# RMSNorm with silu on 16384 rows: hand-placed waits on one program per engine instead of a scheduler

## The chip, the cores and the metric

One core of a Trainium2 chip. The time is device time of the slowest core, here of the only one, in microseconds (us). The kernel before took 185.58 us (median of 3 runs, 185.26 to 185.62). Engines: ACT is ScalarE, DVE is VectorE, POOL is GpSimd, SP only issues transfers and waits. A trailing q ("ACTq") is the engine's queue of issues.

## The reference, cut to what matters

```python
x: (16, 1024, 512) float32, gamma: (512,) float32, eps = 1e-5
rms    = sqrt(mean(x**2, axis=-1, keepdims=True) + eps)
x_norm = x / rms * gamma
return x_norm * (1 / (1 + exp(-x_norm)))
```

The input is 33.55 MB and the output the same. The kernels cut it into 32 tiles of 128 partitions x 4 rows x 512, 1 MB each. A tile is loaded, squared and summed (three of its four rows on ACT, one on DVE), gets rstd = (mean + eps)^-0.5 on GpSimd, is multiplied by rstd and gamma on DVE ("norm"), goes through silu on ACT and is stored.

## The kernel before

The kernel names tiles and dependences; a scheduler puts each engine's instructions in order and places all waits.

```python
lead = 10
xpool = ctx.enter_context(tc.tile_pool(name="xbuf", bufs=20))
...
def load(t):
    x_t = xpool.tile([P, n, D], fp32, name="x_t")
    nc.sync.dma_start(out=x_t[:], in_=xv[t])              # L59
...
def store(t):
    nc.scalar.dma_start(out=ov[t], in_=xt.pop(t)[:])      # L106, on ACT's queue

load(0)
nc.scalar.dma_start(out=gamma_sb[:], in_=gamma.partition_broadcast(P))
for t in range(1, lead):
    load(t)
for k in range(T + 3):
    if k < T:
        stats(k); rstd(k)      # squares: ACT L68, DVE L74; mean: DVE L84; power: POOL L89
    if 0 <= k - 1 < T:
        norm(k - 1)            # DVE L96
    if 0 <= k - 2 < T:
        swish(k - 2)           # ACT L103
        store(k - 2)
    if k + lead < T:
        load(k + lead)
```

## Time and profile before

| | before |
|---|---|
| time, span of the profiled run | 185.58, 183.7 us |
| busy: DVE, ACT, POOL | 60%, 66%, 18% |
| bytes moved | 67.42 MB, of them 0.26 MB gamma |
| mean rate over the span | 367 GB/s |
| rate while the DMA engines are full | 427 GB/s |

No engine is near 100%, and the mean rate is 86% of the full rate. So averages do not tell what bounds this kernel; the slices of the span do, and the prediction shows them. Beside them, the sixth part of the page lists the transfers: the operation, how many, their size, and the median from issue to landing.

```profile
x_t<-in_x_dram SPq DMA_DIRECT2D x32, 1024.0 KB, 20.9
out_dram<-x_t ACTq DMA_DIRECT2D x32, 1024.0 KB, 8.8
```

Loads wait 20.9 us in a long queue, stores 8.8 us in a short one: the DMA engines take packets from both queues, and loads are far ahead.

### The profile page before, as it was taken

What the parts mean: (1) busy time and instruction counts of PE and PEld (TensorE: products, weight loads), DVE (VectorE), ACT (ScalarE), POOL (GpSimd) and SP (SyncE); (2) the same over time, 40 slices, a digit from 0 to 9 for tenths busy, and PEclk for the clock granted to TensorE, in tenths of its full rate; (3) what the DMA queues carried; (4) which work ended last, traced back from release to release, by engine and by line L of the source; (5) the groups of instructions that cost most, each with busy time, mean ns of one, the idle gap of its engine ahead of it and who ended that gap; (6) DMA issues with size and microseconds to landing.
All of it is one profiled execution on the core that took longest, in us unless ns stands there. A gap on an engine that the chain in (4) does not pass through costs nothing.

```text
span 183.7 us, 711 instructions
## 1 busy us (share of the span) xinstructions
DVE 110.7 (60%) x225; ACT 120.9 (66%) x225; POOL 32.8 (18%) x36
## 2 busy tenths in 40 slices
DVE  0177877777725527064443777777777777777650
ACT  2449988842572643168076987999988888888450
POOL 0022322222220201022022222222222222222200
DMA  5999999999999999999999999999985555555195
GB/s 178 338 428 428 425 426 428 423 426 426 428 425 426 423 426 428 425 426 428 428 426 428 428 426 428 428 425 426 425 359 234 228 228 228 228 228 228 57 400 230
DMA packets 9365, 67.42 MB, mean 367 GB/s; under 512 B 1040, under 2 KB 1040, under 8 KB 1168
## 3 DMA queue, kind: packets, MB, share of 16 engines
q10 hardware_dynamic: 4752, 33.82, 44.0%
q1 hardware_dynamic: 4608, 33.56, 44.0%
q14 instruction: 5, 0.04, 0.1%
HBM read 33.82 MB, written 33.55 MB: 367 GB/s over the span
## 4 chain that ended last, share of the span: by engine, by line
DMA 47%; DVE 26%; POOL 9%; issue 9%; ACT 5%; SPq 0%; ACTq 0%; POOLq 0%; DVEq 0%
DMA x_t<-in_x_dram 39%; DVE x_t L96 20%; POOL rstd L89 9%; DMA out_dram<-x_t 7%; DVE sq_dve L74 5%; ACT sq_act L68 3%; ACT x_t L103 2%; DVE aeps L84 1%; SPq L59 0%; ACTq L106 0%; POOLq L89 0%; DVE ms L74 0%; DVEq L96 0%; ACTq L68 0%
## 5 line engine op out<-in xcount | busy, mean ns | idle before, releaser
L96 DVE SCALAR_TENSOR_TENSOR x_t<-x_t,rstd,gamma_sb 128x512 f32<-128x512 f32 x128 | 87.8, 747 | 37.4 <-POOL rstd L89 37.4
L68 ACT ACTIVATE sq_act<-x_t 128x512 bf16<-128x512 f32 x96 | 59.0, 615 | 42.0 <-DMA x_t<-in_x_dram 41.9
L103 ACT ACTIVATE x_t<-x_t 128x2048 f32<-128x2048 f32 x32 | 60.8, 1901 | 15.3 <-DVE x_t L96 13.2
L89 POOL TENSOR_TENSOR rstd<-aeps,neg_half 128x4 f32<-128x4 f32 x32 | 32.6, 1020 | 141.1 <-DVE aeps L84 141.1
L74 DVE CUSTOM_DVE_ANT_0 sq_dve<-x_t 128x512 bf16<-128x512 f32 x32 | 21.9, 685 | 6.3 <-DMA x_t<-in_x_dram 6.3
L84 DVE TENSOR_SCALAR aeps<-ms 128x4 f32<-128x4 f32 x32 | 5.3, 166 | 21.8 <-ACT sq_act L68 21.8
L68 ACT ACTIVATION_READ_ACCUMULATOR sq_act<-x_t 128x1 f32 x96 | 17.9, 186 | 0.0
L74 DVE DVE_READ_ACCUMULATOR2_ANT ms<- 128x1 f32 x32 | 2.6, 83 | 0.0
L44 ACT ACT_TABLE_LOAD x1 | 1.3, 1283 | 0.7 <-PEq L139 0.7
L48 DVE MEMSET neg_half<- 128x4 f32 x1 | 0.1, 62 | 0.8 <-PEq L139 0.8
L139 POOL MEMSET const-float32-0.0<- 128x1 f32 x1 | 0.1, 99 | 0.2 <-issue 0.2
L139 POOL MEMSET const-bfloat16-1.0<- 128x1 bf16 x1 | 0.1, 102 | 0.0
L139 POOL MEMSET const-uint8-127<- 128x1 uint8 x1 | 0.1, 102 | 0.0
L139 POOL MEMSET const-float32-1.0<- 128x1 f32 x1 | 0.1, 99 | 0.0
## 6 DMA issues: line engine op xcount, KB each, us to landing
x_t<-in_x_dram SPq DMA_DIRECT2D x32, 1024.0 KB, 20.9
out_dram<-x_t ACTq DMA_DIRECT2D x32, 1024.0 KB, 8.8
gamma_sb<-in_gamma_dram ACTq DMA_DIRECT2D x1, 256.0 KB, 7.1
```

Of the source, the lines that this page charges most:

```text
L44: nc.scalar.preload_act_table_set("silu_and_others")
L48: nc.vector.memset(neg_half[:], -0.5)
L68: nc.scalar.activation(out=junk[:], in_=x_t[:, j, :], func=AF.Square, accum_out=ms[:, j : j + 1],)
L74: nc.vector.tensor_tensor_reduce(out=junk[:], in0=x_t[:, j, :], in1=x_t[:, j, :], scale=1.0, scalar=0.0, op0=ALU.mult, op1=ALU.add, accum_ ...
L84: nc.vector.tensor_scalar(out=aeps[:], in0=ms[:], scalar1=inv_d, scalar2=eps_f, op0=ALU.mult, op1=ALU.add,)
L89: nc.gpsimd.tensor_tensor(out=r[:], in0=aeps[:], in1=neg_half[:], op=ALU.pow)
L96: nc.vector.scalar_tensor_tensor(out=x_t[:, j, :], in0=x_t[:, j, :], scalar=r[:, j : j + 1], in1=gamma_sb[:], op0=ALU.mult, op1=ALU.mult,)
L103: nc.scalar.activation(out=x_t[:], in_=x_t[:], func=AF.Silu)
L139: nc = _bacc.Bacc("TRN2", target_bir_lowering=False, num_devices=1)
```

## The change

Its intent: take order and waits from the scheduler. Each engine runs one program in order; every slot has a semaphore of its own for its load and one for its store; SP issues loads and stores in alternation; DVE takes the norm of a tile one tile late, so that rstd has time; gamma is loaded into 4 partitions and spread by a shuffle.

```diff
-    lead = 10
+    lead = 8
+    slots = 20
...
+    ld = [tc.alloc_semaphore(f"ld{s}") for s in range(slots)]
+    st = [tc.alloc_semaphore(f"st{s}") for s in range(slots)]
...
     def load(t):
-        x_t = xpool.tile([P, n, D], fp32, name="x_t")
-        nc.sync.dma_start(out=x_t[:], in_=xv[t])
+        if t >= slots:
+            nc.sync.wait_ge(st[t % slots], 16 * (t // slots))
+        nc.sync.dma_start(out=X(t), in_=xv[t]).then_inc(ld[t % slots], 16)
+
+    def store(t):
+        nc.sync.wait_ge(s_swish, t + 1)
+        nc.sync.dma_start(out=ov[t], in_=X(t)).then_inc(st[t % slots], 16)
...
-    def store(t):
-        nc.scalar.dma_start(out=ov[t], in_=xt.pop(t)[:])
...
+        for t in range(lead):
+            load(t)
+        for t in range(T):
+            store(t)
+            if t + lead < T:
+                load(t + lead)
...
+        for t in range(T + 2):          # ACT
+            if t < T:
+                sum_act(t)
+            if t >= 2:
+                swish(t - 2)
+
+        for t in range(T + 1):          # DVE
+            if t < T:
+                sum_dve(t)
+                mean_eps(t)
...
+            if t >= 1:
+                norm(t - 1)
...
+        for s in range(slots):
+            nc.sync.wait_ge(st[s], 16 * ((T - 1 - s) // slots + 1))
```

More of the change, by code (lines that the diff above doesn't have):

```diff
@@ L36 @@
     ov = of.rearrange("(t p n) d -> t p n d", p=P, n=n)
-    consts = ctx.enter_context(tc.tile_pool(name="consts", bufs=1))
-    xpool = ctx.enter_context(tc.tile_pool(name="xbuf", bufs=20))
-    junk_a = ctx.enter_context(tc.tile_pool(name="junk_a", bufs=2))
-    junk_v = ctx.enter_context(tc.tile_pool(name="junk_v", bufs=2))
-    small = ctx.enter_context(tc.tile_pool(name="small", bufs=6))
-    nc.scalar.preload_act_table_set("silu_and_others")
-    gamma_sb = consts.tile([P, D], fp32)
-    neg_half = consts.tile([P, n], fp32)
@@ L48 @@
-    nc.vector.memset(neg_half[:], -0.5)
+    pool = ctx.enter_context(tc.tile_pool(name="all", bufs=1))
+    xb = pool.tile([P, slots, n, D], fp32, name="xb")
+    gamma4 = pool.tile([P, D], fp32, name="gamma4")
+    gamma_sb = pool.tile([P, D], fp32, name="gamma_sb")
+    junk_a = pool.tile([P, n, D], bf16, name="junk_a")
+    junk_v = pool.tile([P, n, D], bf16, name="junk_v")
+    neg_half = pool.tile([P, n], fp32, name="neg_half")
+    ms = pool.tile([P, T, n], fp32, name="ms")
+    aeps = pool.tile([P, T, n], fp32, name="aeps")
@@ L50 @@
+    rstd = pool.tile([P, T, n], fp32, name="rstd")
     inv_d = 1.0 / float(D)
     eps_f = float(eps)
-    xt: dict[int, bass.AP] = {}
-    ms_of: dict[int, bass.AP] = {}
-    rstd_of: dict[int, bass.AP] = {}
-    def load(t):
-        x_t = xpool.tile([P, n, D], fp32, name="x_t")
-        nc.sync.dma_start(out=x_t[:], in_=xv[t])
-        xt[t] = x_t
-    def stats(t):
-        x_t = xt[t]
-        ms = small.tile([P, n], fp32, name="ms")
-        for j in range(n):
-            if j < n_act:
-                junk = junk_a.tile([P, D], bf16, name="sq_act")
-                nc.scalar.activation(
-                    out=junk[:], in_=x_t[:, j, :], func=AF.Square,
-                    accum_out=ms[:, j : j + 1],
-                )
-            else:
-                junk = junk_v.tile([P, D], bf16, name="sq_dve")
-                nc.vector.tensor_tensor_reduce(
-                    out=junk[:], in0=x_t[:, j, :], in1=x_t[:, j, :],
-                    scale=1.0, scalar=0.0, op0=ALU.mult, op1=ALU.add,
-                    accum_out=ms[:, j : j + 1],
-                )
-        ms_of[t] = ms
@@ L81, in rstd @@
-    def rstd(t):
-        ms = ms_of.pop(t)
-        aeps = small.tile([P, n], fp32, name="aeps")
-        nc.vector.tensor_scalar(
-            out=aeps[:], in0=ms[:], scalar1=inv_d, scalar2=eps_f,
-            op0=ALU.mult, op1=ALU.add,
-        )
-        r = small.tile([P, n], fp32, name="rstd")
-        nc.gpsimd.tensor_tensor(out=r[:], in0=aeps[:], in1=neg_half[:], op=ALU.pow)
-        rstd_of[t] = r
-    def norm(t):
-        x_t = xt[t]
-        r = rstd_of.pop(t)
-        for j in range(n):
-            nc.vector.scalar_tensor_tensor(
-                out=x_t[:, j, :], in0=x_t[:, j, :], scalar=r[:, j : j + 1],
+    ld = [tc.alloc_semaphore(f"ld{s}") for s in range(slots)]
@@ new lines, with X @@
+    st = [tc.alloc_semaphore(f"st{s}") for s in range(slots)]
+    g_ld = tc.alloc_semaphore("g_ld")
+    s_const = tc.alloc_semaphore("s_const")
+    s_half = tc.alloc_semaphore("s_half")
+    s_gamma = tc.alloc_semaphore("s_gamma")
+    s_sum_a = tc.alloc_semaphore("s_sum_a")
+    s_sum_v = tc.alloc_semaphore("s_sum_v")
+    s_aeps = tc.alloc_semaphore("s_aeps")
+    s_rstd = tc.alloc_semaphore("s_rstd")
+    s_norm = tc.alloc_semaphore("s_norm")
+    s_swish = tc.alloc_semaphore("s_swish")
+    def X(t):
+        return xb[:, t % slots]
@@ new lines, in landed, with sum_act @@
+    def landed(eng, t):
+        eng.wait_ge(ld[t % slots], 16 * (t // slots + 1))
+    def load(t):
+        if t >= slots:
[4 more added lines that the diff above has]
+        nc.sync.dma_start(out=ov[t], in_=X(t)).then_inc(st[t % slots], 16)
+    def sum_act(t):
+        landed(nc.scalar, t)
+        if t > 0:
+            nc.scalar.wait_ge(s_sum_a, t)
+        for j in range(n_act):
+            ins = nc.scalar.activation(
+                out=junk_a[:, j, :], in_=X(t)[:, j, :], func=AF.Square,
+                accum_out=ms[:, t, j : j + 1],
+            )
+        ins.then_inc(s_sum_a, 1)
@@ new lines, in sum_dve, with mean_eps @@
+    def sum_dve(t):
+        landed(nc.vector, t)
+        if t > 0:
+            nc.vector.wait_ge(s_sum_v, t)
+        for j in range(n_act, n):
+            ins = nc.vector.tensor_tensor_reduce(
+                out=junk_v[:, j, :], in0=X(t)[:, j, :], in1=X(t)[:, j, :],
+                scale=1.0, scalar=0.0, op0=ALU.mult, op1=ALU.add,
+                accum_out=ms[:, t, j : j + 1],
+            )
+        ins.then_inc(s_sum_v, 1)
+    def mean_eps(t):
+        nc.vector.wait_ge(s_sum_a, t + 1)
+        nc.vector.wait_ge(s_sum_v, t + 1)
+        nc.vector.tensor_scalar(
+            out=aeps[:, t, :], in0=ms[:, t, :], scalar1=inv_d, scalar2=eps_f,
+            op0=ALU.mult, op1=ALU.add,
+        ).then_inc(s_aeps, 1)
@@ L98, in norm, with root @@
+    def root(t):
+        nc.gpsimd.wait_ge(s_aeps, t + 1)
+        nc.gpsimd.tensor_tensor(
+            out=rstd[:, t, :], in0=aeps[:, t, :], in1=neg_half[:], op=ALU.pow
+        ).then_inc(s_rstd, 1)
+    def norm(t):
+        nc.vector.wait_ge(s_rstd, t + 1)
+        for j in range(n):
+            ins = nc.vector.scalar_tensor_tensor(
+                out=X(t)[:, j, :], in0=X(t)[:, j, :], scalar=rstd[:, t, j : j + 1],
                 in1=gamma_sb[:], op0=ALU.mult, op1=ALU.mult,
             )
+        ins.then_inc(s_norm, 1)
@@ L101, in swish @@
     def swish(t):
-        x_t = xt[t]
-        nc.scalar.activation(out=x_t[:], in_=x_t[:], func=AF.Silu)
-    def store(t):
-        nc.scalar.dma_start(out=ov[t], in_=xt.pop(t)[:])
-    load(0)
-    nc.scalar.dma_start(out=gamma_sb[:], in_=gamma.partition_broadcast(P))
-    for t in range(1, lead):
-        load(t)
-    for k in range(T + 3):
-        if k < T:
-            stats(k)
-            rstd(k)
-        if 0 <= k - 1 < T:
-            norm(k - 1)
-        if 0 <= k - 2 < T:
-            swish(k - 2)
-            store(k - 2)
-        if k + lead < T:
-            load(k + lead)
+        nc.scalar.wait_ge(s_norm, t + 1)
@@ new lines, in swish @@
+        nc.scalar.activation(out=X(t), in_=X(t), func=AF.Silu).then_inc(s_swish, 1)
+    with tc.tile_critical():
+        for t in range(lead):
[4 more added lines that the diff above has]
+                load(t + lead)
+        nc.gpsimd.memset(gamma4[:], 0.0).then_inc(s_const, 1)
+        nc.scalar.wait_ge(s_const, 1)
+        nc.scalar.dma_start(
+            out=gamma4[0:P:32, :], in_=gamma.partition_broadcast(4)
+        ).then_inc(g_ld, 16)
+        nc.scalar.preload_act_table_set("silu_and_others")
+        nc.gpsimd.memset(neg_half[:], -0.5).then_inc(s_half, 1)
+        nc.gpsimd.wait_ge(s_half, 1)
+        for t in range(T + 2):
[7 more added lines that the diff above has]
+                mean_eps(t)
+            if t == 0:
+                nc.vector.wait_ge(g_ld, 16)
+                nc.vector.stream_shuffle(gamma_sb[:], gamma4[:], [0] * 32).then_inc(s_gamma, 1)
+            if t == 1:
+                nc.vector.wait_ge(s_gamma, 1)
+            if t >= 1:
+                norm(t - 1)
+        for t in range(T):
+            root(t)
+        for s in range(slots):
+            nc.sync.wait_ge(st[s], 16 * ((T - 1 - s) // slots + 1))
```

## The prediction

> **What bounds the kernel now.** I read the page first, for where the time is not used. Its second part, the busy shares in 40 slices of 4.6 us:
>
> ```profile
> DVE  0177877777725527064443777777777777777650
> ACT  2449988842572643168076987999988888888450
> DMA  5999999999999999999999999999985555555195
> GB/s 178 338 428 428 425 426 428 423 426 426 428 425 426 423 426 428 425 426 428 428 426 428 428 426 428 428 425 426 425 359 234 228 228 228 228 228 228 57 400 230
> ```
>
> Three stages can be seen. Slices 0 and 1 are the start. In slices 2 to 28, up to about 133 us, the DMA engines are full at some 427 GB/s while both compute engines have holes, worst in slices 8 to 20. From slice 29 on the DMA engines are half empty at 228 GB/s and ACT and DVE are at 70 to 80%. So the kernel is first bound by transfers and then by compute, and the compute lost in the first stage is paid for in the last one. At 427 GB/s the 67.42 MB of the page's third part need 157.9 us; the other 26 us of the 183.7 us span are the start and the half-empty tail.
>
> Next the chain of work that ended last. In its middle:
>
> ```profile
> 31.44 23.19 DMA x_t<-in_x_dram
> 54.65 19.03 DMA x_t<-in_x_dram
> ...
> 74.16 23.56 DMA x_t<-in_x_dram
> 97.72 0.02 issue
> 97.76 0.04 issue
> 97.80 0.34 ACTq L106
> 98.14 0.05 issue
> 98.19 0.78 ACT sq_act L68 x3
> ```
>
> A load issued at 74.16 us lands at 97.72 us; what it releases is not the squares of its own tile but the *issue of a store* on ACT's queue (L106) at 97.80, and the squares (L68) come behind it. No data ties that store to that load. The instruction order explains it: the scheduler has only eight DMA semaphores, deals them out to loads and stores in turn, and lets each DMA wait until the previous DMA with its semaphore has landed. A store behind a load on the same semaphore holds ACT's in-order queue until that load lands. I went through the trace's landing times: the store issued at 66.37 us follows a load landing at 66.30, the one at 58.70 a load at 58.62, the one at 51.34 a load at 51.27. The view of waits sums this up:
>
> ```profile
> ACT sq_act L68 <- DMA x_t<-in_x_dram: 41.9, 13, 6.7
> ...
> DVE aeps L84 <- ACT sq_act L68: 21.8, 8, 5.8
> ```
>
> The 41.9 us "of ACT for loads" are, but for the first wait of some 5 us and one of 1 us, waits of a store for a semaphore and not for data: at 44 us eleven loads had landed and only six tiles were swished. Meanwhile loads run ahead to fill 20 buffers, so the DMA stays full but with the wrong half of its work: all loads have landed at 125.97 us, when about half of the stores are still to come.
>
> Last, what paces the tail. One period of the same chain:
>
> ```profile
> 147.76 2.07 DVE x_t L96 x3
> 149.83 0.60 DVE sq_dve L74
> 150.44 0.10 DVE aeps L84
> 150.54 0.02 issue
> 150.58 0.09 issue
> 150.67 1.02 POOL rstd L89
> 151.69 0.02 issue
> 151.71 0.04 DVE x_t L96
> ```
>
> The chain comes round every 4.62 us: DVE asks GpSimd for rstd of a tile and at once needs it for the norm of the *same* tile, so DVE idles about 1.2 us per tile (37.4 us in 32 waits over the kernel). One 1 MB store per 4.62 us is the 228 GB/s of the tail.
>
> **What the Trainium skill says.** "DMA: Bandwidth & Descriptors", section "Issuing engines are not separate DMA queues", says that DMAs started by SP and by ACT run on the same 16 DMA engines, and a second issuing engine saves issue time only. The trace agrees: loads alone (slices 2 and 3), both queues, and stores alone (landing every 2.4 to 2.8 us from 126 to 139 us) all move about 427 GB/s. So putting the stores on SP's queue should cost no bandwidth. The same page, "Where 436 GB/s comes from", derives a ceiling of 435.2 GB/s; 428 is 98% of it, so I expect no faster transfers, only fuller use. Its "Rules for kernel authors" advise a dedicated semaphore for a DMA, which is what the change does; the 41.9 us show what sharing costs here. All durations below come from the trace.
>
> **The change part by part.**
>
> *Semaphores per slot, stores issued by SP.* Removed: every wait of a DMA on an unrelated one. Loads now wait for the store that freed their slot 12 tiles earlier (long landed), stores for their own swish. ACT loses 32 store issues of 0.34 us and the roughly 36 us of false waits.
>
> *Order fixed by hand.* On DVE it is now sum(t), mean(t), norm(t-1), so rstd has about a period to come: the 1.2 us wait goes. DVE per tile: 0.685 (sum) + 0.17 (mean) + 4 x 0.69 (norms back to back, 2.74 in the timeline) = 3.6 us. ACT: three squares and one silu back to back took 3.63 us (21.14 to 24.77 us in the timeline); with hand-placed waits I take 3.7 to 3.9. Both are below the 1.0486 MB x 2 / 427 GB/s = 4.91 us that one load and one store need, so compute stops being a bound in every stage and the transfers must set the pace throughout.
>
> *Lead 8, load t+8 issued behind store t on one queue.* This binds loads to stores, so that they can't run ahead. Is 8 enough? Eight periods are 39.3 us. A tile spends on compute: two periods until tile t+2 has landed (ACT takes the squares of t+2 before the silu of t), 9.8 us, plus 1.9 and 1.9 us for these two, 13.6 us. About 25.7 us remain as queueing of a transfer, some ten transfers deep: the queue never runs dry. At the start eight loads fill it until about 25 us, and store 0 comes at about 17 us. At the end load 31 is the 56th of 64 transfers, lands near 142 us, and leaves eight stores, 19.6 us; its own compute needs about 10 us. The last store is ready near 153 us, before its turn at 159. So the engines should be full from about 9 us to the end.
>
> *Gamma.* 256 KB become 8 KB: 0.25 MB / 427 GB/s = 0.6 us of DMA less. In its place stand a GpSimd fill and a shuffle on DVE, under a microsecond or so each by the length of their 128x512 output, in the 7 us before the first tile or beside tile 0: nothing on the path.
>
> *Sum.* In the kernel before, load 5 landed at 20.02 us; six loads were then moved, plus gamma. 58 transfers of 2.456 us follow: 142.4 us. 20.0 + 142.4 - 0.6 = 161.8 us for the last landing. Before, the last store landed at 182.78 us and the span ended 0.9 us later: 162.7. I add 0.8 us for the barrier around the hand-written part and the slower completion of a store in a full queue (an estimate by feel): span 163.5 us. The timed value stands 1.9 us over the span (185.58 against 183.7): **165.4 us**, 11% less. The gain of 20 us consists of the tail: it was 54 us at about 228 GB/s, moving what 29 us at 427 would, 25 us lost, of which the last tile's compute and landing were never avoidable in full.
>
> **Rivals.** (1) *One ring is worse than two.* Loads and stores in alternation in one ring have not been seen in this trace; a turn between reading and writing HBM could cost. Against it: packets of both queues alternated in the first stage at 427 GB/s, each taking the same 309 ns. If each transfer lost 0.1 us, 64 x 0.1 = 6 us: 172 us. (2) *The queue's depth.* At most eight DMAs were outstanding before; now about ten would be in one ring. If SP blocks when the ring is full, it blocks with the DMA engines busy, so the time stays at 165 us; only landing times would be shorter than my 25 us. (3) *Compute becomes the bound.* If hand-placed waits drain ACT or DVE, a tile would have to cost 4.9 us instead of 3.8 before it shows; at 5.2 us per tile, 32 x 5.2 plus 10 us of start and 5 of end are 181 us. The self-waits number two or three per tile and cannot plausibly make 1.1 us. (4) *DMA was full already.* Reading only the first 29 slices, one would say that removing waits buys nothing: 185 us. Against it stands the tail, in which the engines are half idle.
>
> **Range and chances.** Below the 157.2 us of pure transfer plus the 5 us of start and 2 of launch lies nothing: the low end is 164.0. Rival 1 in a mild form gives the high end, 170.0. Faster by over 2% needs less than 181.9 us, which only rivals 3 and 4 in full miss: 0.96; within 2% 0.03; slower 0.01.
>
> **What would show it.** Right: about 427 GB/s in every slice from the third to the last but one; DMA share of the slices 9 throughout; all bytes on SP's queue (some 67.1 MB); loads and stores alike landing some 25 us after issue; DVE waiting for rstd hardly at all (below 5 us in place of 37.4); squares waiting some 1.2 us per tile, for their own load; silu busy until about 153 us with only stores after it. Wrong: slices below 415 GB/s in the middle (rival 1), DMA slices of 7 or 8 with ACT at 9 (rival 3), or a last stage of stores at less than full rate.

## The result, and the profile after

The changed kernel takes 166.81 us (median of 4 runs, 166.74 to 167.47), beside 185.42 us for the kernel before (now with a fourth run): a ratio of 0.9006, 95% interval 0.8978 to 0.9033.

The busy shares of the changed kernel in 40 slices, now of 4.1 us:

```profile
DVE  0269999999996666786666776666876666784000
ACT  3488999999977977777977758877778977777000
DMA  4999999999999999999999999999999999999990
GB/s 157 415 425 429 425 342 429 411 431 427 427 431 419 431 423 433 423 431 425 429 427 427 423 425 431 421 435 419 435 423 431 425 425 431 421 433 423 433 405 26
```

The three stages have become one. DMA is at 9 from the second slice to the last but one, loads and stores mixed. The compute engines are full only up to slice 10 or 11, while they work off the first loads, and then follow the transfers, DVE at 60 to 80% and ACT at 70 to 90%. The last load lands at 142.84 us, so from slice 35 on there are stores alone, at full rate.

One of the waits of the kernel before (engine and line, what it waited for, us in total, times, longest), and the longest two of ACT and DVE in the changed kernel:

```profile
DVE x_t L96 <- POOL rstd L89: 37.4, 32, 1.2
```

```profile
DVE aeps L107 <- ACT junk_a L86: 28.9, 26, 1.3
ACT junk_a L86 <- DMA xb<-in_x_dram: 26.9, 23, 2.0
```

DVE's wait for rstd, 37.4 us before, is not in the list of the changed kernel any more. ACT still waits for loads, 26.9 us, but 2.0 us at most at a time, and now for data of the tile it is about to square. One period of the timeline shows this (start, duration, engine, line, operation, then idle time before it and its releaser):

```profile
87.11 0.34 SPq L79 DMA_DIRECT2D out_dram<-xb  x1
87.50 1.42 SPq L75 DMA_DIRECT2D xb<-in_x_dram  x1
88.25 0.63 ACT L86 ACTIVATE junk_a<-xb 128x512 bf16<-128x512 f32 x1 [1.17 <-DMA xb<-in_x_dram]
...
90.10 1.89 ACT L129 ACTIVATE xb<-xb 128x2048 f32<-128x2048 f32 x1
90.23 0.17 DVE L107 TENSOR_SCALAR aeps<-ms 128x4 f32<-128x4 f32 x1 [1.28 <-ACT junk_a L86]
90.31 2.73 DVE L121 SCALAR_TENSOR_TENSOR xb<-xb,rstd,gamma_sb 128x512 f32<-128x512 f32 x4
90.48 1.44 POOL L114 TENSOR_TENSOR rstd<-aeps,neg_half 128x4 f32<-128x4 f32 x1 [3.48 <-DVE aeps L107]
92.02 0.34 SPq L79 DMA_DIRECT2D out_dram<-xb  x1
```

A store goes out every 4.9 us (87.11, 92.02), the time of two transfers. The norms (L121) start right behind the mean with no idle, because they use the rstd of the tile before. The power on GpSimd now takes 1.44 us against 1.01 to 1.02 us before. The Trainium skill, "SBUF — State Buffer", section "Who interferes with whom", says that a DVE instruction with two SBUF inputs contends with a GpSimd instruction that reads SBUF; the trace agrees in direction, as the norms have two inputs in SBUF and now run beside it (with the order undone, in old_dve_order below, the power's mean is back at 1.01 us). It has a whole period to end, so it costs nothing.

### The profile page after: what moved, and what is told of

Same layout as the page of the kernel before. It is cut to its first block, busy times and chain, and to the rows that moved or that the text cites. A ratio compares the mean times of both kernels' runs of the same rounds, so it can differ in the third digit from the quotient of the medians.

```text
span 165.0 us, 713 instructions
## 1 busy us (share of the span) xinstructions
DVE 112.0 (68%) x226; ACT 120.5 (73%) x225; POOL 46.4 (28%) x38
## 4 chain that ended last, share of the span: by engine, by line
DMA 63%; ACT 17%; issue 6%; DVE 5%; SPq 1%
DMA xb<-in_x_dram 63%; ACT junk_a L86 12%; ACT xb L129 6%; DVE xb L121 5%; SPq L79 1%; SPq L75 0%; DVE aeps L107 0%; SPq L203 0%; SPq L131 0%
## 5 line engine op out<-in xcount | busy, mean ns | idle before, releaser
L121 DVE SCALAR_TENSOR_TENSOR xb<-xb,rstd,gamma_sb 128x512 f32<-128x512 f32 x128 | 87.4, 745 | 0.0
L86 ACT ACTIVATE junk_a<-xb 128x512 bf16<-128x512 f32 x96 | 59.2, 617 | 26.9 <-DMA xb<-in_x_dram 26.9
L114 POOL TENSOR_TENSOR rstd<-aeps,neg_half 128x4 f32<-128x4 f32 x32 | 45.7, 1427 | 99.4 <-DVE aeps L107 99.4
L129 ACT ACTIVATE xb<-xb 128x2048 f32<-128x2048 f32 x32 | 60.6, 1895 | 2.2 <-DVE xb L121 2.2
L97 DVE CUSTOM_DVE_ANT_0 junk_v<-xb 128x512 bf16<-128x512 f32 x32 | 22.0, 689 | 8.7 <-DMA xb<-in_x_dram 6.8
L86 ACT ACTIVATION_READ_ACCUMULATOR junk_a<-xb 128x1 f32 x96 | 17.9, 186 | 0.0
L162 DVE STREAM_SHUFFLE gamma_sb<-gamma 128x512 f32<-128x512 f32 x1 | 0.7, 717 | 0.0
L141 POOL MEMSET gamma<- 128x512 f32 x1 | 0.5, 524 | 0.5 <-PEq L203 0.5
## 6 DMA issues: line engine op xcount, KB each, us to landing
xb<-in_x_dram SPq DMA_DIRECT2D x32, 1024.0 KB, 23.2
out_dram<-xb SPq DMA_DIRECT2D x32, 1024.0 KB, 22.4
```

The costliest lines, as they stand in the source:

```text
L86: ins = nc.scalar.activation(out=junk_a[:, j, :], in_=X(t)[:, j, :], func=AF.Square, accum_out=ms[:, t, j : j + 1],)
L97: ins = nc.vector.tensor_tensor_reduce(out=junk_v[:, j, :], in0=X(t)[:, j, :], in1=X(t)[:, j, :], scale=1.0, scalar=0.0, op0=ALU.mult, op1 ...
L114: nc.gpsimd.tensor_tensor(out=rstd[:, t, :], in0=aeps[:, t, :], in1=neg_half[:], op=ALU.pow).then_inc(s_rstd, 1)
L121: ins = nc.vector.scalar_tensor_tensor(out=X(t)[:, j, :], in0=X(t)[:, j, :], scalar=rstd[:, t, j : j + 1], in1=gamma_sb[:], op0=ALU.mult, ...
L129: nc.scalar.activation(out=X(t), in_=X(t), func=AF.Silu).then_inc(s_swish, 1)
L141: nc.gpsimd.memset(gamma4[:], 0.0).then_inc(s_const, 1)
```

## The experiments

Theory A is the prediction's: waits of stores on shared semaphores, standing in ACT's queue, starved compute and pushed stores into a tail. Theory B: the limit of eight shared semaphores hurts wherever its waits stand. Theory C: DVE's order, with its wait for rstd, carries the gain. Theory D: binding loads to stores on one queue does.

### The same waits put back, and the order on DVE undone: two by two

From the trace before I read which earlier transfer had each transfer's semaphore. With S for a store and L for a load: S3 waits for L6, S5 for L10, S7 for L14, S9 for L19, S12 for L25. So *a store had to wait until about twice as many loads had landed*. The next kernel puts exactly these waits into the changed kernel, with stores on ACT's queue and loads bound only by the slots and by these waits, on the new DVE order. The edit of **lanes_back**:

```diff
+    STORE_AFTER = {1: gamma, 2: L3, 3: L6, 4: L8, 5: L10, ... 12: L25, ...}
+    LOAD_AFTER = {6: L0, 7: L1, ... 10: S0, 11: L5, 12: S1, ...}
     def load(t):
+        lane(nc.sync, LOAD_AFTER, t)
     def store(t):
+        lane(nc.scalar, STORE_AFTER, t)
-        nc.sync.wait_ge(s_swish, t + 1)
-        nc.sync.dma_start(...)
+        nc.scalar.wait_ge(s_swish, t + 1)
+        nc.scalar.dma_start(...)
-        for t in range(lead): load(t)
-        for t in range(T): store(t); load(t + lead)
+        for t in range(T): load(t)
```

Each store is issued behind the first square of the third tile after it, as the scheduler had it.

> The changed kernel with the suspected cost put back and the new DVE order kept: stores on ACT's queue, loads free to run ahead, and each DMA waits for the same earlier DMA as the scheduler's eight semaphores made it wait in the kernel before (so store 12 waits until load 25 has landed). Theory A: the run-ahead and the store-only tail come back; with the tail paced by ACT and DVE at about 4.0 us per tile instead of 4.6 I expect 176 to 183 us. Theory C: 166 to 169 us, since the DVE order is the new one.

Measured 174.91 us, ratio 0.9436 to before (0.9422 to 0.945). ACT's shares and the rates in its 40 slices of 4.3 us:

```profile
ACT  2589999160817528034808597799999999999640
GB/s 174 423 421 421 338 425 429 427 427 423 429 423 429 429 433 425 423 427 425 427 427 433 425 427 425 427 427 423 427 427 427 395 283 242 302 316 312 280 363 123
```

And from its waits:

```profile
ACT junk_a L109 <- DMA xb<-in_x_dram: 42.3, 14, 6.7
```

The picture of before is back: holes in ACT beside full DMA engines, 42.3 us in 14 waits (41.9 in 13 before), and a tail of stores. The tail moves about 290 GB/s instead of 228, since in it a store goes out every 3.64 us instead of 4.62. The time is 1 us under my range, which had 4.0 us per tile there: the issue of a store on ACT did not lengthen its period.

The other single undoing is **old_dve_order**, on the changed kernel:

```diff
-        for t in range(T + 1):
-            if t < T: sum_dve(t); mean_eps(t)
-            if t >= 1: norm(t - 1)
+        for t in range(T):
+            sum_dve(t); mean_eps(t)
+            norm(t)
```

> The changed kernel with one part undone: on DVE the norm of tile t follows its own mean at once, so that DVE waits for rstd again, some 1.0 to 1.4 us per tile and 32 to 45 us in all. Theory A: hidden under the transfers, 166.5 to 169 us. Theory C (the DVE order carries the gain): 178 us or more.

Measured 169.67 us, ratio 0.9152 (0.9136 to 0.9167). DVE waits for rstd again, and nearly all of it is hidden:

```profile
DVE xb L121 <- POOL rstd L114: 35.4, 32, 1.1
```

In this run the middle slices keep 419 to 435 GB/s. My range was 0.7 us too low. Stores went out every 4.75 us, too close to the 4.89 us of the transfers, so at the end the last stores come at that pace and not from a waiting queue; the last one was issued at 161.59 us instead of 152.27.

Both together, **lanes_and_old_order** (the two edits above):

> Both put back into the hand-written kernel: the waits of the eight semaphores and the old DVE order. If these two account for all of the difference, this runs like the kernel before: 183 to 188 us. If it stays below 180 us, something else of the rewriting (barriers, gamma, buffers) carries part of the gain.

Measured 188.57 us, ratio 1.0171 (1.0156 to 1.0186), half a microsecond over my range and 3 us over the kernel before. So these two parts account for all of the difference (and 3 us more, which the hand-written order of this corner costs against the scheduler's; I did not take them apart):

| us | new DVE order | old DVE order |
|---|---|---|
| own semaphores | 166.81 | 169.67 |
| waits of the eight semaphores | 174.91 | 188.57 |

Taking out the waits gains 18.9 us on the old order (188.57 - 169.67) and 8.1 us on the new one; the order gains 13.7 us with the waits and 2.9 us without. The sum of the single gains from the worst corner, 32.6 us, is far over the 21.8 us of both: each removes much of the other's cost. That is what a tail paced by compute means. The waits decide how much is left for the tail, and the order decides how fast the tail runs. (The lower row also has the stores on ACT's queue and the loads untied from the stores. free_loads below shows that these two cost nothing on the new order; on the old one they were not tried without the waits.) Theory C alone falls.

### One word changed in the scheduled kernel

**before_stores_on_sp**, on the kernel before:

```diff
     def store(t):
-        nc.scalar.dma_start(out=ov[t], in_=xt.pop(t)[:])
+        nc.sync.dma_start(out=ov[t], in_=xt.pop(t)[:])
```

> The scheduled kernel of before, with one word changed: its stores are issued by SP instead of ACT. The eight shared DMA semaphores stay, but their waits now stand in one in-order queue with the loads, and ACT has no wait of a store in front of its squares. Theory A (the false waits of stores on ACT's queue are the cause): DMA full throughout, 166 to 170 us, because the old DVE order at 4.6 us per tile still fits under the 4.89 us that a load and a store need. Theory B (the eight shared semaphores limit it wherever they wait): above 178 us. Theory C (DVE's wait for rstd is the cause): above 178 us, since DVE keeps its wait.

Measured 212.22 us, ratio 1.1447 (1.143 to 1.1464): slower than before by 27 us, and theory A's number for it was badly wrong. Its rates in 40 slices of 5.3 us:

```profile
GB/s 188 372 425 425 422 422 422 427 428 427 427 427 427 427 431 424 428 425 427 428 428 428 427 427 425 427 81 150 199 199 75 125 199 75 125 199 199 111 90 199
```

And its waits:

```profile
ACT x_t L103 <- DVE x_t L96: 77.7, 28, 4.2
DVE aeps L84 <- ACT sq_act L68: 49.3, 16, 3.2
...
ACT sq_act L68 <- DMA x_t<-in_x_dram: 6.1, 2, 5.0
```

The false waits are gone as theory A has it (6.1 us in place of 41.9, and only two). In their place ACT and DVE wait for each other, 127 us in the first two lines. The instruction order shows why: with the store off its queue, the scheduler chose another order on ACT. Before, the silu of a tile stood behind the squares of the tile two places on; here, from tile 12 on, most silus stand right behind the squares of their own tile. Then nothing overlaps: squares, mean, power, norm and silu follow each other, and a tile takes 7.9 us. One period of its timeline:

```profile
159.40 1.91 ACT L103 ACTIVATE x_t<-x_t 128x2048 f32<-128x2048 f32 x1 [4.16 <-DVE x_t L96]
161.22 0.61 ACT L68 ACTIVATE sq_act<-x_t 128x512 bf16<-128x512 f32 x1
...
163.18 0.17 DVE L84 TENSOR_SCALAR aeps<-ms 128x4 f32<-128x4 f32 x1 [3.20 <-ACT sq_act L68]
163.49 1.01 POOL L89 TENSOR_TENSOR rstd<-aeps,neg_half 128x4 f32<-128x4 f32 x1 [6.90 <-DVE aeps L84]
164.54 2.74 DVE L96 SCALAR_TENSOR_TENSOR x_t<-x_t,rstd,gamma_sb 128x512 f32<-128x512 f32 x4 [1.19 <-POOL rstd L89]
...
167.31 1.91 ACT L103 ACTIVATE x_t<-x_t 128x2048 f32<-128x2048 f32 x1 [4.16 <-DVE x_t L96]
```

From silu to silu 167.31 - 159.40 = 7.91 us. So the edit was not the clean one that I took it for: one word changed two things. Two more kernels separate them.

**scheduler_act_order** puts only that order into the changed kernel:

```diff
+        ahead = [2, 2, 3, 3, 3, 3, 3, 3, 3, 3, 3, 2, 1, 2, 1, 1,
+                 1, 1, 2, 1, 1, 1, 1, 2, 1, 1, 1, 1, 2, 1, 1, 1]
+        squared = 0
+        for t in range(T):
+            while squared < min(T, t + ahead[t]):
+                sum_act(squared); squared += 1
+            swish(t)
-        for t in range(T + 2):
-            if t < T: sum_act(t)
-            if t >= 2: swish(t - 2)
```

with the old DVE order of above.

> The changed kernel, all its semaphores and its queue kept, with the orders that the scheduler chose on ACT and DVE when the stores were moved to SP: DVE takes the norm of a tile right behind its mean, and from tile 11 on ACT takes most silus right behind the squares of the same tile. If this order alone made the 212 us of the scheduled kernel with its stores on SP, this one takes 205 to 214 us. If the eight shared semaphores made it, this one stays below 185 us.

Measured 216.06 us, ratio 1.1657 (1.1641 to 1.1673), 2 us over my range. ACT waits 80.4 us for DVE and DVE 49.3 us for ACT, with each slot's own semaphore in place. So the order is enough to make the 212 us, without any shared semaphore.

**eight_in_flight** puts only the limit of eight into the changed kernel:

```diff
+    def eight_back():
+        if len(done) >= 8:
+            nc.sync.wait_ge(*done[-8])   # the transfer eight places before has landed
     def load(t):
+        eight_back()
     def store(t):
+        eight_back()
```

> The changed kernel with at most eight transfers in flight: each DMA on SP's queue also waits until the one eight places before it has landed, as eight semaphores dealt out in order would have it. The instruction order of ACT and DVE stays. Theory A: eight transfers are 19.6 us of work, the queue stays full and no engine but SP waits, 166.5 to 168.5 us. Theory B (eight shared semaphores limit it wherever the wait stands, as the 212 us of the scheduled kernel with its stores on SP might suggest): above 178 us.

Measured 166.52 us, ratio 0.8983 (0.8968 to 0.8998), as fast as the changed kernel. SP's own waits:

```profile
SPq L83 <- DMA xb<-in_x_dram: 36.9, 19, 2.1
SPq L89 <- DMA out_dram<-xb: 36.7, 18, 2.9
```

SP now waits 74 us in these two lines for earlier transfers, and no time is lost, because no compute stands behind it and seven to eight transfers keep the DMA engines full. Theory B falls: eight semaphores are enough; what hurts is a wait on them in the queue of a compute engine.

### Loads set free

**free_loads** is lanes_back without its waits: stores on ACT's queue, loads as far ahead as the 20 slots allow.

```diff
-        lane(nc.sync, LOAD_AFTER, t)
-        lane(nc.scalar, STORE_AFTER, t)
```

> The changed kernel with stores on ACT's queue again and loads not tied to stores: a load waits only for its slot, so up to 20 may run ahead of the stores, as in the kernel before, but without the waits of the eight semaphores. Theory A (only the false waits made the loads run ahead at the cost of the stores): still full to the end, 166 to 169 us. Theory D (binding load t+8 to store t on one queue is what keeps the tail full): 174 us or more.

Measured 166.51 us, ratio 0.899 (0.8968 to 0.9012), and the tail is full:

```profile
GB/s 151 424 428 428 325 418 432 418 432 420 436 420 436 420 436 416 440 416 436 420 436 420 430 422 426 428 428 426 426 430 424 432 424 432 424 430 426 428 384 14
```

The loads did run ahead, 15 of them issued before store 0 and 24 before store 10. No load waited for a slot; what held them was their own issue, which took up to 13.56 us. Theory D falls: loads that *may* run ahead do no harm, as the DMA engines then serve both queues and compute keeps up. Only loads that *must* be ahead before a store may go do harm. Against lanes_back the waits alone cost 8.4 us.

### How much lead is needed

**lead_5** and **lead_4** change one number, `lead = 8` to 5 and to 4.

> The changed kernel with 5 loads ahead of the first store instead of 8. From a silu to the silu three tiles later: 0.8 us for two issues, some 6 us until the load behind the store has landed on an empty queue, 3.9 us for squares and silu, together 10.4 to 10.7 us, or 3.5 us per tile, below the 4.89 us of the transfers. So 166.5 to 169 us. If the lead were already short at 8, this would be far slower, 175 us or more.

> The same with 4 loads ahead: the same 10.4 to 10.7 us now has to do for two tiles, 5.2 to 5.35 us per tile, above the 4.89 us of the transfers, so the DMA engines run dry for a part of each period: 176 to 186 us. If it stays at 167 us the loop is shorter than I work it out.

Measured 169.38 us, ratio 0.9143 (0.9123 to 0.9163), for 5, 0.4 us over my range, and 192.49 us, ratio 1.0374 (1.0345 to 1.0404), for 4, 6.5 us over my range and slower than the kernel before. With 5, the middle keeps 423 to 434 GB/s, and the loss is at the start (slices of 335 and 288 GB/s) and in the last stores. With 4, the loop is the bound, and longer than I worked out:

```profile
82.92 0.34 SPq L79 DMA_DIRECT2D out_dram<-xb  x1
83.30 0.43 SPq L75 DMA_DIRECT2D xb<-in_x_dram  x1
...
94.04 0.34 SPq L79 DMA_DIRECT2D out_dram<-xb  x1
```

Two tiles take 94.04 - 82.92 = 11.1 us, 5.6 us per tile, where I had 5.2 to 5.35. The load behind a store takes 6.9 to 7.5 us from its issue to landing and not 6, and ACT then needs 3.9 us.

### Gamma and the end

**gamma_full** loads gamma as before, without fill and shuffle:

```diff
-        nc.gpsimd.memset(gamma4[:], 0.0).then_inc(s_const, 1)
-        nc.scalar.wait_ge(s_const, 1)
         nc.scalar.dma_start(
-            out=gamma4[0:P:32, :], in_=gamma.partition_broadcast(4)
+            out=gamma_sb[:], in_=gamma.partition_broadcast(P)
         ).then_inc(g_ld, 16)
...
-                nc.vector.stream_shuffle(gamma_sb[:], gamma4[:], [0] * 32)...
```

> The changed kernel with gamma loaded as 256 KB into all partitions, as before, and without fill and shuffle. By bytes, 0.25 MB at 427 GB/s: 0.6 us more, 167.3 to 167.6 us. The rival is that it hides in the slow start and the time stays within 0.2 us of the changed kernel.

Measured 168.18 us, ratio 0.9075 (0.9063 to 0.9088): 1.4 us more than the changed kernel, over twice what its bytes need and 0.6 us over my range. The first load lands at 7.49 us instead of 5.88. Packets of 8 KB usually take 309 ns; what those over 345 ns took beyond 309 adds up, in the first 10 us, to 0.96 us per DMA engine, against 0.46 us in the changed kernel and 1.25 us in the kernel before. But the changed kernel has 0.64 us more of it between 21 and 33 us, where gamma_full has none, so over the whole run the two are alike (1.19 and 1.14 us), and slow packets do not explain the difference.

The landings tell more. A transfer raises its semaphore in 16 steps, whose times the trace has. I take each step to be one of the 16 DMA engines that has done its share: at the end of gamma_full the last four packets of 8 KB end about 0.31 us apart (162.98, 163.29, 163.60, 163.90 us), as from one engine that works alone. At the last store the median of the 16 steps came at 161.96 us in gamma_full and at 161.35 us in the changed kernel: 0.6 us later, as the bytes ask. The last step came at 164.23 and 162.47 us: the slowest engine was 2.3 us behind the median in gamma_full and 1.1 us in the changed kernel. The rest of the loss in these two profiled runs is thus the larger lag of the slowest engine. Whether the gamma load causes it is not shown: three kernels with the small gamma load lag by 1.2 us (eight_in_flight), 1.7 us (end_waits) and 1.9 us (free_loads).

**end_waits** reorders the last waits and has fewer slots:

```diff
-    slots = 20
+    slots = 14
...
-        for s in range(slots):
-            nc.sync.wait_ge(st[s], 16 * ((T - 1 - s) // slots + 1))
+        for t in range(T - slots, T):
+            nc.sync.wait_ge(st[t % slots], 16 * (t // slots + 1))
```

> The changed kernel with its last waits in the order in which the stores land and with 14 slots instead of 20. After the last landing at 162.47 us SP went through ten waits of 0.06 us, and the clearing of the semaphores took 0.34 us against 0.10 before. So 0.6 us for the waits and 0.1 us for the 12 semaphores less: 165.9 to 166.3 us. Slots are freed 29 us after a store is issued, which lands within 24 us, so 14 slots should not bind; if they do, the middle slices fall below 420 GB/s.

Measured 166.36 us (166.18 to 166.68), ratio 0.8972 (0.896 to 0.8984), the lowest time. The last waits now end 0.1 us after the last landing, and from that landing to the end of the span pass 1.9 us instead of 2.5. Against 166.81 us of other rounds the time is 0.4 us less, about as much as runs differ, so I call the gain no more than likely. The 14 slots do not bind.

## Why the prediction was right or wrong

The time was within the range, 1.4 us above the point, and the direction was right. By its steps:

- *Bound by transfers, then by compute; false waits starve ACT.* Right, and shown: lanes_back brings holes and tail back, free_loads without the waits has neither. One sentence was loose. It says that loads "run ahead to fill 20 buffers" meanwhile; in fact the waits force them ahead, as store 12 needs load 25 landed.
- *Semaphores per slot and stores on SP.* The gain was right, its place only half. SP's queue is not needed (free_loads has the stores on ACT), nor is the number of semaphores (eight_in_flight). Needed is that no unrelated transfer stands before a store in ACT's order.
- *Order by hand.* Right that the 1.2 us per tile go and that compute ceases to be a bound: DVE's wait for rstd went from 37.4 us to none. The prediction added both parts into one gain and did not say that they overlap; the table of two by two has 18.9 and 13.7 us alone and 21.8 together.
- *Lead 8 behind the store "binds loads to stores, so that they can't run ahead".* The binding was unnecessary: 166.51 us without it. That 8 is enough was right; 5 costs 2.6 us and 4 costs 25.7 us.
- *Gamma, 0.6 us.* Right for the bytes, as the median DMA engine shows; mis-sized as a whole: 1.4 us by gamma_full, with the slowest engine lagging further behind.
- *The sum.* Predicted 161.8 us for the last landing, 163.5 for the span, 165.4 timed; measured 162.47, 165.0 and 166.81. Two terms were mis-sized. The start was better: seven loads had landed at 20.92 us, where the working gives 20.0 + 2.456 - 0.6 = 21.9. The 57 transfers after it took 141.55 us, 2.483 us each and not 2.456, or 1.5 us more. Some 0.6 us of it are slow packets between 21 and 33 us, where the sixth slice falls to 342 GB/s; another 0.8 us is the slowest DMA engine, which fell from 0.3 us behind the median at the seventh load to 1.1 us at the last store. The sum took all 16 engines as equal. And from the last landing to the end passed 2.5 us, where I had 0.9 + 0.8: ten waits of SP one after the other (0.6 us), the exit of the hand-written part, and the clearing of more semaphores.
- *Rival 1, one ring worse than two.* Refuted: 411 to 435 GB/s in every slice from the seventh to the last but two, and 166.51 us with two queues. Its sign, a slice below 415, did show in the sixth (342) and the eighth (411), but free_loads with two queues has the same dip (325). *Rival 2, the queue's depth.* It came in the harmless form named: with ten transfers outstanding a load's issue took 0.46 to 2.00 us (median 1.13), where with five to nine it took 0.43 to 0.57, with the DMA engines full. Landing times were 23.2 us for loads and 22.4 us for stores in the median, against the 25 predicted. *Rivals 3 and 4* are refuted by the result.

What stays open: why packets are slow around the first stores in the hand-written kernels with the small gamma load, and in neither the kernel before nor gamma_full; and why some DMA engines fall behind the others.

## What to carry to other kernels

When DMA engines are full while compute has holes, ask whether they move the right half of the work: a store that waits for an unrelated load leaves a tail that a mean DMA share does not show. Look at what stands *before* the idle instruction in its engine's order, as the profile puts a wait on the next instruction it counts as busy; an issue of a transfer in a compute engine's queue is a likely place. And a scheduler answers a small edit with a new order on all engines, so compare orders before you draw a conclusion from a time.

## What the Trainium skill lacked or had wrong

- "DMA: Bandwidth & Descriptors" gives no number of transfers that one queue takes before its issuer is held. Here, with 1 MB transfers, a load's issue on SP rose in the changed kernel from 0.43 to 0.57 us, with five to nine outstanding, to a median of 1.13 us (up to 2.00) once ten were; with up to 14 outstanding over two queues a load's issue took up to 13.56 us. With eight or fewer it stayed at 0.33 to 0.80 us in all runs.
- The table of measured rates on the same page has loads alone, and I found no page with a rate on this chip for stores from SBUF to HBM. Here loads and stores in alternation on one queue, and then stores alone, ran at 411 to 435 GB/s in every slice from the second to the last but two, but for the sixth (342). The page's ceiling of 435.2 GB/s held as a mean over longer stretches (427 GB/s over 20 us).
- The same page's ground for a semaphore of its own for each DMA in flight is correctness (stale reads, in "Why a DMA increments its semaphore by 16 and not by 1"); it lacks the cost in time of sharing, which depends on where the wait stands: 8.4 us on ACT's queue (lanes_back against free_loads), nothing on SP's (eight_in_flight, which has the same limit of eight).
- No page says what a small load on a second queue takes from a stream of large ones: 1.4 us here for 256 KB, which need 0.6 us. Nor does any say how far the DMA engines drift apart in a full stream: at the last store the slowest was 1.1 to 2.3 us behind the median of the 16 (five runs), against 0.1 us in the kernel before, whose last stores found the engines half empty.
